# Output projection as one stage of all tokens, scaled up operands in DRAM, up products chained in PSUM, and an FFN without seams between its pieces

## The chip, the cores and the metric

One core of a Trainium2 chip runs the whole layer as one program. The metric is device microseconds of that core per execution; lower is better. The profile is of one execution, taken on the same core, and lists what every engine did: PE (matrix multiply; PEld is its weight load), DVE and ACT (elementwise work), POOL (GpSimd, elementwise work that cannot touch PSUM) and SP (which issues the DMAs).

## The reference

2048 prompt tokens and 32 sample tokens of width 1024 go through one layer, in float32:

```
n = rmsnorm(x);  z = n @ w_in
A = sliding-window attention with sinks,  B = gated linear attention (GLA)
h = x + concat(A, B) @ w_out                       # 1024 x 1024
y = h + relu(rmsnorm(h) * g_ffn @ w_up)^2 @ w_down # 1024 x 4096, 4096 x 1024
```

It also returns the last keys, values and GLA states.

## The kernel before

Every float32 matrix is split into a high part and the rest (h and l), and each product is three matmuls (`mm3`: h·h, h·l, l·h). Everything is transposed: channels lie on partitions and tokens on the free axis.

The program has an attention stage (`attention_phase`), a GLA stage (`gla_phase`) and an FFN stage (`ffn_phase`). Their order on PE is the program's order; tasks of the first two stages are interleaved by a clock of estimated PE time (`spawn`, `tick`). DMAs are issued from SP, in order, and an issue that waits holds those behind it.

The FFN stage works on three pieces of tokens with two groups each: 2 x 328, 2 x 356, 2 x 356. Both products of the FFN are done as 2 x 2 blocks with seven products instead of eight (Strassen-Winograd). The tokens' blocks are B11, B21 (group 0, channel halves), B22 and the differences T1 to T4; the weights' are A11, A12, A22 and sums S1 to S4. The hidden width of 4096 is cut into NF = 16 blocks of 256. Per block there are seven up products (`product`, 12 matmuls each), the relu and square, new differences of the hidden blocks (`uT1` to `uT4`), and seven down products (`down`, 12 matmuls each into two PSUM tiles, added by DVE to accumulators in SBUF at L1320). Down product i of block b-1 and up product i of block b alternate.

Per piece, in order: the output projection of its two groups (`op`, 192 matmuls per group; the first group of the first piece is done at the end of the GLA stage, in `prepare_ffn`), residual add, sums of squares, splitting into operands (`pair`), the 16 blocks, and then merges of the accumulators (`combine`, L1575) and stores. The RMS scale of each token is applied after the up products, in one DVE operation (L1488: max with 0, times scale). Each up product has its own PSUM tile, and DVE makes the sums and differences of products (L1320 with `r0`, `r1`, `r2`).

Weight pairs: `weights` (L1208) makes h on ACT and l on POOL from a staged load, for a ring of eight tiles, AHEAD = 7 steps before use. Pairs of w_down (and block 0 of w_up) are written to DRAM in the first piece and read back in the others; those of w_up are remade in every piece, with four POOL operations per block for the block sums (L1234). The output weights' pairs are written to DRAM once (L1305) and read in the two later pieces. In the later pieces POOL also makes five of the seven low parts of the hidden blocks (L1481).

The block sums of w_down are made ahead of the FFN by POOL (`down_sums`, L687 to L698): blocks 0 to 7 in the attention stage from its third tile on, blocks 8 to 15 in the GLA stage, in two tasks that load, add, store at once and then wait.

## Time and profile before

| | us |
|---|---|
| median of 3 runs (2425.57 to 2433.79) | 2426.84 |
| profiled execution | 2427.7 |
| its span, first to last instruction | 2425.7 |
| PE busy | 2211.6 |
| DVE busy | 1871.4 |
| POOL busy | 1426.5 |
| ACT busy | 1009.5 |
| mean granted TensorE clock | 0.960 of full |
| DMA | 437.49 MB, 180 GB/s |

Busy shares are averages over stages with different limits, so a stage is read by its own row, and a wait by what ended it. A line number is that of the kernel before; L42 and L135 are helpers through which all ACT operations and all matmuls go, so their groups are told apart by tile names: `dn` is a down product, `PS1T`, `PA12B` and the like are up products, `op` the output projection, `fB` hidden blocks, `sd` sums of w_down, `wf` weight pairs.

### The profile page before, as it was taken

How to read it: one execution, taken by the hardware profiler on the slowest of the kernel's cores; microseconds unless marked ns; L12 is line 12 of the kernel's file. 1: busy time of each engine (PE TensorE's matmuls, PEld its weight loads, DVE VectorE, ACT ScalarE, POOL GpSimd, SP SyncE). 2: the span in 40 equal slices, each digit the busy share in tenths (PEclk: the TensorE clock that was granted, in tenths of full speed). 3: DMA queues.
4: the chain of work that ended last, by engine and by line, in shares of the span. 5: the costliest groups of instructions: out<-in, count | busy, mean ns of one | idle time of the engine just before them, and what ended most of it. 6: DMA issues, size and time to landing. Idle time of an engine off the chain costs nothing.

```text
span 2425.7 us, 40665 instructions
## 1 busy us (share of the span) xinstructions
PE 2211.6 (91%) x14790; PEld 2038.2 (84%) x14790; DVE 1871.4 (77%) x3637; ACT 1009.5 (42%) x2197; POOL 1426.5 (59%) x1360
## 2 busy tenths in 40 slices
PE   7999999969988899999989799999999899999996
PEld 6776777758877789988889799999998789999995
DVE  8666766868985788888885578888886578888887
ACT  4444556536554544444442433333331443333331
POOL 6553225752333588887882366666674166666773
PEclk9999999889989899999999899999999899999998
DMA  9564455543157466565687355555558445555544
GB/s 304 185 204 149 163 176 180 191 163 110 61 195 227 153 220 228 217 217 217 217 300 240 114 168 166 163 163 163 165 165 250 155 153 165 158 164 157 165 133 133
DMA packets 259625, 437.49 MB, mean 180 GB/s; under 512 B 46289, under 2 KB 172546, under 8 KB 255586
## 3 DMA queue, kind: packets, MB, share of 16 engines
q1 hardware_dynamic: 259426, 434.90, 54.1%
q8 instruction: 117, 1.92, 0.3%
q14 instruction: 82, 0.67, 0.1%
HBM read 307.70 MB, written 127.13 MB: 179 GB/s over the span
## 4 chain that ended last, share of the span: by engine, by line
PE 51%; DVE 19%; POOL 11%; DMA 8%; issue 5%; ACT 4%; SPq 1%; DVEq 0%; ACTq 0%; POOLq 0%
PE dn L135 15%; DVE fB L1320 7%; PE op L135 6%; POOL stage L1234 4%; PE PA22T L135 3%; PE PS3T L135 3%; PE PS2T L135 3%; PE PS1T L135 3%; PE zv L135 3%; PE zq L135 3%; PE zr L135 2%; DMA sd<-sd 2%; DVE P L1320 2%; DMA sd<-in_w_down 2%; DVE y L1320 2%
## 5 line engine op out<-in xcount | busy, mean ns | idle before, releaser
L1320 DVE TENSOR_TENSOR y<-y,dn 128x712 f32<-128x712 f32 (+1 forms) x384 | 330.3, 868 | 11.9 <-PE dn L135 5.7
L1234 POOL TENSOR_TENSOR stage<-stage 128x512 f32<-128x512 f32 x184 | 249.0, 1353 | 12.1
L1320 DVE TENSOR_TENSOR P<-P,dn 128x712 f32<-128x712 f32 (+1 forms) x270 | 235.0, 871 | 27.1 <-PE dn L135 21.9
L1320 DVE TENSOR_TENSOR fB<-fB,fB 128x356 f32<-128x356 f32 (+1 forms) x192 | 204.2, 1063 | 4.9 <-ACT fB L42 2.9
L687 POOL TENSOR_TENSOR sd<-sd 128x128 f32<-128x128 f32 (+1 forms) x192 | 117.5, 628 | 66.4 <-DMA sd<-in_w_down 55.3
L912 POOL TENSOR_TENSOR E<-cc 128x256 f32<-128x256 f32 (+1 forms) x117 | 68.1, 621 | 81.4 <-DVE cc L764 79.6
L988 DVE COPY_PREDICATED AT<-masks,A 64x64 f32<-64x64 int32 (+1 forms) x330 | 82.6, 252 | 38.9 <-ACT AT L42 29.5
L1335 DVE TENSOR_TENSOR op<-op,y 128x356 f32<-128x356 f32 (+1 forms) x48 | 23.7, 523 | 84.2 <-PE op L135 36.0
L1346 POOL TENSOR_TENSOR sums<-sums,r 128x356 f32<-128x356 f32 (+1 forms) x9 | 8.4, 934 | 126.3 <-DVE sums L1346 85.8
L42 ACT ACTIVATE P<-S,negm 128x192 f32<-128x192 f32 (+2 forms) x128 | 51.6, 417 | 51.7 <-DVE negm L556 41.0
L1481 DVE TENSOR_TENSOR uT1l<-fB,uT1h 128x356 fp32r<-128x356 f32 (+1 forms) x48 | 69.7, 1452 | 0.0
L42 ACT ACTIVATE E<-E 128x1024 f32<-128x1024 f32 (+2 forms) x68 | 67.2, 1013 | 1.1
L1320 DVE TENSOR_TENSOR PA22T<-PA22T,r 128x356 f32<-128x356 f32 (+1 forms) x48 | 25.3, 527 | 53.0 <-PE PA22T L135 52.9
L42 ACT ACTIVATE y<-op 128x356 f32<-128x356 f32 (+1 forms) x48 | 22.3, 466 | 105.1 <-DVE op L1335 78.2
L42 ACT ACTIVATE uT2h<-fB 128x356 fp32r<-128x356 f32 (+1 forms) x48 | 23.6, 492 | 92.5 <-DVE fB L1320 92.5
L135 PE MATMUL op<-T3h,wf_o 128*128 128x356 f32 x128 | 38.4, 373 | 21.9 <-DVE T4l L1327 21.9
L923 DVE TENSOR_TENSOR E<-E,kq 128x256 f32<-128x256 f32 (+1 forms) x117 | 55.0, 522 | 2.0 <-ACT E L42 1.9
L42 ACT ACTIVATE uT1h<-fB 128x356 fp32r<-128x356 f32 (+1 forms) x48 | 23.8, 495 | 78.6 <-DVE fB L1320 78.6
L1320 DVE TENSOR_TENSOR r<-PS1T,r 128x356 f32<-128x356 f32 (+1 forms) x48 | 24.8, 516 | 41.1 <-PE PS1T L135 41.1
L1320 DVE TENSOR_TENSOR r<-PS3T,r 128x356 f32<-128x356 f32 (+1 forms) x48 | 24.8, 518 | 39.2 <-PE PS3T L135 39.2
L311 DVE TENSOR_TENSOR xT1a<-xT1a,packed 128x512 f32<-128x512 f32 (+2 forms) x36 | 22.4, 666 | 40.8 <-DMA xT1a<-in_xT_prompt 40.8
L42 ACT ACTIVATE fB<-PS1T 128x356 f32<-128x356 f32 (+1 forms) x48 | 22.1, 461 | 71.7 <-DVE PS1T L1488 71.7
(1861 smaller groups left out, 8864.4 us busy)
## 6 DMA issues: line engine op xcount, KB each, us to landing
stage<-in_w_up SPq DMA_DIRECT2D x92, 512.0 KB, 4.9
stage<-sd SPq DMA_DIRECT2D x32, 512.0 KB, 7.2
wf_o<-ko SPq DMA_DIRECT2D x32, 512.0 KB, 6.1
xT1a<-in_xT_prompt SPq DMA_DIRECT2D x16, 512.0 KB, 4.3
stage<-in_w_in SPq DMA_DIRECT2D x16, 512.0 KB, 5.3
sd<-in_w_down SPq DMA_DIRECT2D x64, 128.0 KB, 3.1
x1a<-in_x_prompt SPq DMA_DIRECT2D x16, 512.0 KB, 5.0
sd<-sd SPq DMA_DIRECT2D x32, 256.0 KB, 3.0
```

Source lines behind the costliest of these rows:

```text
L42: ins = f(*args, **kw)
L135: self._pe(self.T.matmul(out, lhsT, rhs, start=start, stop=stop), ns)
L311: V.tensor_tensor(out=xT[:, ks], in0=xT[:, ks], in1=self.gmix[:, ks].unsqueeze(2).broadcast_to([P, step, r]), op=ALU.mult)
L687: tt = lambda o, x, y, op: self.G.tensor_tensor(out=o, in0=x, in1=y, op=op)
L912: G.tensor_tensor(out=e4, in0=c4, in1=ref, op=ALU.subtract)
L923: V.tensor_tensor(out=e4, in0=e4, in1=halves_of(kq, L, m), op=ALU.mult)
L988: V.copy_predicated(dst, mk.unsqueeze(1).broadcast_to([L // nh, 2, w // m, m]), src[r].rearrange("s p (n m) -> s p n m", m=m),)
L1234: tt = lambda o, x, y, op: G.tensor_tensor(out=o, in0=x, in1=y, op=op)
L1320: tt = lambda out, x, y, op=ALU.add: V.tensor_tensor(out=out, in0=x, in1=y, op=op)
L1335: V.tensor_tensor(out=ps, in0=ps, in1=yf, op=ALU.add)
L1346: (G if pool else V).tensor_tensor(out=acc, in0=acc, in1=sq, op=ALU.add)
L1481: (G if pool else V).tensor_tensor(out=l, in0=src, in1=f32(h), op=ALU.subtract)
```

## The change

The output projection of all six groups becomes a stage of its own (`op_phase`) between GLA and FFN, with the output weights kept in SBUF. For each group it adds x, stores h to DRAM (`yd`), sums squares and, one group later (`post`), multiplies h by gain and scale, forms B11 to T4 and stores them to DRAM (`Td`). The same stage makes the sums of w_down for blocks 13 to 15 and sums of w_up for blocks 1 to 8, which it keeps in DRAM (`su`).

The FFN runs 3 x 16 blocks in one sequence, pieces in the order 1, 2, 0. Operands of the next piece are loaded and split (`load_tok`) as each up product of a piece's last block has been issued. Up products 0, 2, 4 and 6 accumulate in one PSUM bank (X) and 3 and 5 in another (W); ACT copies out what is needed in between. The RMS scale is already in the operands, so the relu is an ACT operation. All low parts of hidden blocks are made by DVE. The down order becomes A11, S4, S1, S3, S2, A12, A22. The residual h is loaded and added by POOL during blocks 2 to 9. Merges move partly into the last two blocks, and in pieces that are not the last they are on POOL.

Weight pairs of w_down are remade in every piece (only block 15 is kept, and block 0 of w_up as before); in the first piece two of seven are on DVE. Up sums that are kept are loaded instead of made; for blocks 9 to 15 the first half is kept in the first piece. The output weights are no longer written to DRAM.

`down_sums`: five blocks in the attention stage, from its tenth tile on, eight in the GLA stage; the store waits for the second pause and is put behind the DMA issued last before it.

```diff
--- before.py
+++ after.py
-EARLY = 8
-AHEAD = 7
+ORDER = (1, 2, 0)
+EARLY, MIDDLE = 5, 8
+AHEAD = 6
...
+        self.su = [[dt([P, KB // 2, 256], f"su{b}{j}") for j in range(2)] for b in range(self.NB)]
+        self.made = {}
+        self.Td = [
+            {x: dt([P, KB // 2, n], f"Td{p}{x}") for x in ("B11", "B21", "T2", "T1", "T3", "B22", "T4")}
+            for p, n in enumerate(sizes)
+        ]
...
-                if i == 2:
+                if i == 9:
...
-            a11, a21, a12, a22 = raw[:, 0, 0], raw[:, 0, 1], raw[:, 1, 0], raw[:, 1, 1]
-            tt(a22, a21, a22, ALU.add)
-            tt(a21, a11, a21, ALU.subtract)
-            tt(a11, a22, a11, ALU.subtract)
-            tt(a12, a12, a11, ALU.subtract)
-            self.Q.dma_start(self.sd[b][:, :, c0 : c0 + n], raw.rearrange("p k m n -> p (k m) n"))
+            self.block_sums(raw)
             yield gap / 2
+            with self.tc.issue_after(self.Q.last.ins):
+                self.Q.dma_start(self.sd[b][:, :, c0 : c0 + n], raw.rearrange("p k m n -> p (k m) n"))
...
-            late = [(b, c0, 256) for b in range(EARLY, self.NB) for c0 in (0, 256)]
+            late = [(b, c0, 256) for b in range(EARLY, EARLY + MIDDLE) for c0 in (0, 256)]
...
+        def post(p, gi, acc):
...
+            sc = rb[:, :N]
+            scaled = lambda out, f: V.scalar_tensor_tensor(out=out, in0=y[:, f], scalar=g(f), in1=sc, op0=ALU.mult, op1=ALU.mult)
+            Td = self.Td[p]
+            if gi == 0:
+                for f in range(KB):
+                    scaled(y[:, f], f)
+                    if f == H - 1:
+                        Q.dma_start(Td["B11"], y[:, :H])
+                Q.dma_start(Td["B21"], y[:, H:])
+                return
+            A, B = pa[:, :N], pb[:, :N]
...
+            for k in range(H):
+                scaled(A, k)
+                scaled(y[:, H + k], H + k)
+                tt(t3[:, k], y[:, H + k], A)
+                tt(A, A, y0[:, k])
+                S.activation(y[:, k], A, AF.Copy)
+                tt(B, y[:, H + k], A)
+                S.activation(t2[:, k], B, AF.Copy)
+                tt(t4[:, k], y0[:, H + k], B)
+            for x, src in (("T2", t2), ("T1", y[:, :H]), ("T3", t3), ("B22", y[:, H:]), ("T4", t4)):
+                Q.dma_start(Td[x], src)
...
+        todo, raws = [("d", b, c) for b in range(EARLY + MIDDLE, self.NB) for c in (0, 256)], []
+        todo += [("u", b, 0) for b in range(1, 9)]
...
+        for j, (p, gi) in enumerate(groups):
...
+            for f in range(KB):
+                if j == 0:
+                    ps = self.op0[f]
+                else:
+                    ps = self.ps_s(f"op{p}_{gi}_{f}")[:, :N]
+                    for kb in range(KB):
+                        w = [self.wo[f // H][kb // 4][x][:, kb % 4, cs] for x in range(2)]
+                        self.mm3(ps, *w, mix[p, gi](kb, 0), mix[p, gi](kb, 1), kb == 0, kb == KB - 1)
+                V.tensor_tensor(out=y[:, f], in0=ps, in1=y[:, f], op=ALU.add)
+                S.activation(ps if f else acc, y[:, f], AF.Square)
+                if f:
+                    V.tensor_tensor(out=acc, in0=acc, in1=ps, op=ALU.add)
+                if f % H == H - 1:
+                    hs = slice(f - H + 1, f + 1)
+                    Q.dma_start(self.yd[p][gi][:, hs], y[:, hs])
+                if f in (1, 2) and pending is not None:
+                    next(pending, None)
+                if f == (0 if gi else 2) and j + 1 < len(groups):
+                    load_y(*groups[j + 1])
+                if f == 1 and 2 <= j + 1 < len(groups):
+                    next_mix(*groups[j + 1])
+                if j and f in (1, 3, 5, 7):
+                    sums()
+            pending = post(p, gi, acc)
+        self.pending = pending
...
+            wring = [(wfb, i) for i in range(5)] + [(wfa, 0), (wfa, 1), (wfc, 0)]
...
+            def load_tok(e, x, engs):
+
+                h, l = e.T[x]
+                Q.dma_start(f32(l), self.Td[e.p][x])
+                for i, eng in enumerate(engs):
+                    ks = slice(i * H // len(engs), (i + 1) * H // len(engs))
+                    S.activation(h[:, ks], f32(l[:, ks]), AF.Copy)
+                    eng.tensor_tensor(out=l[:, ks], in0=f32(l[:, ks]), in1=f32(h[:, ks]), op=ALU.subtract)
...
+                def product(ps, i, first=False):
+
+                    w, t = UP[i]
+                    wh, wl = (x.rearrange("p (k c) -> p k c", k=H) for x in ws["U", g].pop(w))
+                    th, tl = e.T[t]
+                    for kb in range(H):
+                        self.mm3(ps, wh[:, kb], wl[:, kb], th[:, kb], tl[:, kb], first and kb == 0, kb == H - 1, skip_group_check=not first)
+                    if b == NF - 1 and n + 1 < len(envs):
+                        load_tok(envs[n + 1], t, (G, G))
...
+                X = bank(bx)
+                product(X, 0, True)
+                S.activation(r0, X, AF.Copy)
+                yield
+                Z = bank(bz)
+                product(Z, 1, True)
+                add(Z, Z, r0)
+                squared("B11", Z, f1)
+                yield
+                product(X, 2)
+                S.activation(r2, X, AF.Copy)
+                yield
+                W = bank(3)
+                product(W, 3, True)
+                S.activation(r5, W, AF.Copy)
+                yield
+                product(X, 4)
+                Y = bank(by)
+                add(Y, X, r5)
+                squared("B22", Y, f3)
+                yield
+                product(W, 5)
+                add(W, W, r2)
+                S.activation(W, W, AF.Relu)
+                S.activation(W, W, AF.Square)
+                add(Y, W, f1, ALU.subtract)
+                add(W, f3, W, ALU.subtract)
+                split("T1", Y)
+                split("T3", W)
+                add(W, W, f1)
+                split("T2", W)
+                yield
+                product(X, 6)
+                squared("B21", X, r5)
+                add(X, r5, W, ALU.subtract)
+                split("T4", X)
...
+            for x, g, i in steps:
+                if x == "U":
+                    if i == 0:
+                        ups[g] = up(g)
+                    next(ups[g])
+                    if g == 0 and i in (0, 2):
+                        next(self.pending, None)
+                else:
+                    down(g, i)
+                    n, b = divmod(g, NF)
+                    e, end = envs[n], n + 1 == len(envs)
+                    residual(g, i)
+                    if b == NF - 2 and i == 2:
+                        merge(e, 3, 5, False)
+                    if b == NF - 2 and i == 4:
+                        merge(e, 6, 1, False)
+                        merge(e, 2, 1, False)
+                    if b == NF - 1 and i == 4:
+                        merge(e, 3, 6, end)
+                        store(e, 3)
+                        merge(e, 7, 6, end)
+                        merge(e, 5, 7, end)
+                        store(e, 5)
+                    if b == NF - 1 and i == 5:
+                        store(e, 2)
+                    if b == NF - 1 and i == 6:
+                        merge(e, 4, 7, end)
+                        store(e, 4)
+                prepare()
```

More of the change, by code (lines that the diff above doesn't have):

```diff
@@ new lines, in up_weights, with fetch @@
+                raw = [None, None]
+                def fetch(k):
+                    raw[k] = load(w[:, H * k : H * k + H, 256 * b : 256 * b + 256])
+                half = lambda x, m: x[:, :, m * P : m * P + P]
+                tt = lambda o, x, y, op: G.tensor_tensor(out=o, in0=x, in1=y, op=op)
+                made = self.made.get(b, 0)
+                fetch(0)
+                if made < 2:
+                    fetch(1)
+                a11, a21 = half(raw[0], 0), half(raw[0], 1)
+                pair("A11", a11)
@@ L1242, in up_weights @@
+                yield
+                if made == 2:
+                    fetch(1)
+                a12, a22 = half(raw[1], 0), half(raw[1], 1)
+                sums = [load(x) for x in self.su[b][:made]]
+                pair("A12", a12)
                 yield
-                pair("A22", A(2, 2))
-                tt(A(2, 2), A(2, 1), A(2, 2), ALU.add)
-                if not b:
-                    pair("S1", A(2, 2))
+                if made:
+                    s2, s3 = half(sums[0], 0), half(sums[0], 1)
+                    pair("S2", s2)
@@ L1283, in down_weights @@
                 made = f"d{b}A11" in kept
+                src = {}
                 for i, (x, _, _) in enumerate(DOWN):
                     if not made and i == 0:
-                        fetch(0)
-                    if not made and i % 2 and i + 1 < 7:
-                        fetch(i + 1)
-                    out[x] = weights(f"d{b}{x}", lambda: halves[x], True)
-                    yield
-            def out_weights(fh):
-                kbs = []
-                for kb in range(KB):
-                    key = f"o{fh}{kb}"
-                    kbs.append(weights(key, None, True))
-                return kbs
@@ new lines, in down_weights @@
+                        src["A11"] = load(w_dn[b, :, 0:1, :512], True)
+                        s = load(self.sd[b][:, 2:4], True)
+                        src["S4"], src["S1"] = s[:, 0:1], s[:, 1:2]
+                    if not made and i == 2:
+                        s = load(self.sd[b][:, :2], True)
+                        src["S2"], src["S3"] = s[:, 0:1], s[:, 1:2]
+                    if not made and i == 4:
+                        s = load(w_dn[b, :, 1:2, :], True)
+                        src["A12"], src["A22"] = s[:, :, :512], s[:, :, 512:]
@@ new lines, in down_weights @@
+                    eng = V if n == 0 and i in (0, 5) else G
+                    out[x] = weights(f"d{b}{x}", None if made else src[x], keep, eng)
+                    yield
+            steps = [("U", 0, i) for i in range(7)]
+            total = len(envs) * NF
+            for g in range(1, total):
+                steps += [(x, g - (x == "D"), i) for i in range(7) for x in "DU"]
+            steps += [("D", total - 1, i) for i in range(7)]
+            ws, makers = {}, {}
+            todo = iter(steps)
@@ L1593, in ffn_phase, with merge @@
-                combine(6, 1)
-                combine(7, 6)
-                combine(6, 5)
-                combine(5, 7)
-                store(1, range(H, KB))
-                combine(3, 6)
-                store(1, range(H))
-                combine(4, 7)
-                store(0, range(H, KB))
-                if pi + 1 < len(pieces):
-                    y = [load_y(pi + 1, gi) for gi in range(2)]
+                            V.tensor_copy(at, ps)
+            def merge(e, q, x, last):
+                for j in range(0, H, 2):
+                    eng = V if last and j else G
+                    eng.tensor_tensor(out=e.acc[q][:, j : j + 2], in0=e.acc[q][:, j : j + 2], in1=e.acc[x][:, j : j + 2], op=ALU.add)
```

666 lines of the change are left out of this document (293 added, 373 removed).

## The prediction

> **What bounds the kernel now.** I read the busy shares, then the span cut by stage, then the chain of waits in one steady block, then waits by pair and single durations.
>
> ```profile
> span 2425.7 us, 40665 instructions
> PE 2211.6 (91%) x14790; PEld 2038.2 (84%) x14790; DVE 1871.4 (77%) x3637; ACT 1009.5 (42%) x2197; POOL 1426.5 (59%) x1360
> ```
>
> PE is the busiest engine, but where its idle time lies matters more than the 91%. The span by stage (columns: stretch, length, busy time of PE, weight loads, DVE, ACT, POOL, granted clock, DMA share, GB/s):
>
> ```profile
> core 0: us, PE busy (x) PEld busy (x) DVE busy (x) ACT busy (x) POOL busy (x), PEclk, DMA share, GB/s
> 505.00:530.00 25.00, 4.29 (x116) 3.35 (x114) 4.55 (x12) 3.47 (x9) 10.94 (x15) 0.66 0.66 225
> 690.00:718.00 28.00, 20.93 (x195) 18.03 (x193) 25.20 (x70) 16.12 (x27) 9.79 (x4) 0.76 0.88 293
> 797.90:1278.00 480.10, 436.16 (x2716) 420.46 (x2715) 417.08 (x605) 224.47 (x453) 391.74 (x293) 0.96 0.62 223
> 1278.00:1363.70 85.70, 72.23 (x392) 70.31 (x393) 39.83 (x65) 25.07 (x56) 20.79 (x17) 0.88 0.53 169
> 1363.70:1847.80 484.10, 458.03 (x2722) 445.25 (x2721) 395.19 (x522) 168.94 (x334) 326.56 (x266) 0.98 0.54 171
> 1847.80:1928.50 80.70, 68.80 (x394) 67.86 (x393) 41.48 (x67) 25.15 (x56) 12.25 (x8) 0.92 0.52 172
> 1928.50:2407.70 479.20, 455.10 (x2712) 441.36 (x2710) 393.18 (x519) 161.98 (x318) 312.08 (x252) 0.99 0.50 158
> 2407.70:2425.70 18.00, 0.03 (x1) 0.00 (x0) 10.59 (x7) 0.00 (x0) 9.41 (x5) 0.58 0.38 122
> 1427.15:1456.26 29.11, 27.89 (x168) 27.27 (x169) 24.27 (x32) 9.73 (x19) 20.05 (x16) 1.00 0.52 164
> 1875.00:1899.80 24.80, 24.80 (x153) 24.50 (x151) 15.18 (x29) 13.62 (x32) 0.00 (x0) 1.00 0.61 235
> ```
>
> The rows are: a hole in the GLA stage; its end; then FFN, seam (the output projection of a piece), FFN, seam, FFN; the tail; one steady block; the densest stretch of a seam. Clock and holes go together: stretches with PE nearly full are granted 1.00, those with holes 0.66 to 0.92, so a hole costs itself and a slow restart.
>
> Inside a steady block the chain of waits runs through products back to back, then leaves PE:
>
> ```profile
> 1516.86 1.95 PE PS2T L135 x12
> ```
> ```profile
> 1530.69 0.65 ACT wf_u6A L42
> 1531.41 1.31 POOL wf_u6A L1208
> 1532.79 1.31 POOL stage L1234
> 1534.16 1.29 POOL stage L1234
> 1535.46 0.92 POOL uB22l L1481
> 1536.38 1.62 DVE fB L1320
> ...
> 1542.67 0.51 ACT uT2h L42
> ```
> ```profile
> PE dn L135 <- ACT uT2h L42: 17.0, 14, 1.2
> ```
> ```profile
> PE dn L135 <- DVE y L1320: 29.3, 27, 2.2
> ```
> ```profile
> 902.98 1.81 PE dn L135 x12
> ```
>
> Twelve matmuls of 356 columns take 1.95 us, of 328 columns 1.81 us. A block is 14 such products, 27.3 us dense, but its period is 29.11: weight copy on ACT, four GpSimd operations, DVE differences, uT2, and PE waits 1.2 us for it (14 blocks: 17.0). In the first piece the wait is for DVE's accumulation (29.3 in 27 waits).
>
> **The change, part by part.** Base: from the first matmul of the second output group to the last product, all PE work as if back to back.
>
> ```profile
> 753.86 0.41 PE L135 MATMUL op<-m1h,wo00h 128*128 128x328 f32 x1 [0.53 <-ACT op L42]
> ```
> ```profile
> 1381.17 2.02 PE rb L135 x8
> ```
>
> The number of matmuls is unchanged. FFN: 2 x 16 x 27.3 + 16 x 14 x 1.81 = 1279.0. Five output groups of 16 twelves each: 4 x 31.2 + 29.0 = 153.8. The row-scale broadcasts, now six: 6 x 2.02 = 12.1. With 753.9 in front: 2198.8. Before, the same work ended at 2407.7, so 209 us of holes are at stake, and the tail.
>
> *Up products chained, scale moved to the tokens.* DVE did 17 operations per block in later pieces (22 in the first), among them two-SBUF ones:
>
> ```profile
> L1320 DVE TENSOR_TENSOR y<-y,dn 128x712 f32<-128x712 f32 x256 | 224.9, 889 | 8.3 <-PE dn L135 2.6
> ...
> L1320 DVE TENSOR_TENSOR fB<-fB,fB 128x356 f32<-128x356 f32 x128 | 140.8, 1100 | 4.5 <-ACT fB L42 2.9 <-POOL B22l L1083 1.3
> ...
> L1320 DVE TENSOR_TENSOR PA22T<-PA22T,r 128x356 f32<-128x356 f32 x32 | 17.2, 537 | 36.1 <-PE PA22T L135 36.1
> ...
> L1575 POOL TENSOR_TENSOR y<-y,P 128x356 f32<-128x356 f32 x8 | 14.0, 1773 | 1.4 <-DVE y L1320 1.3
> ```
>
> Now it does 14, each with a PSUM operand: 14 x 0.537 + 14 x 0.889 = 20.0 us of 27.3. A difference with both operands in SBUF took 1100 ns, one with a PSUM operand 537. The Trainium skill (SBUF — State Buffer, "Who interferes with whom") says that a DVE instruction with two SBUF inputs and a GpSimd instruction that reads SBUF exclude each other for the whole instruction, and that one SBUF input does not contend; the two rows agree, and by that rule alone the in-block waits below would be nothing and the result 29 us lower.
> ACT: 21 operations at the 0.51 of uT2 + 14 weight copies x 0.65 = 19.8 us. GpSimd: 14 low parts x 1.31 = 18.3, up to 5.2 for block sums and 3.7 for the residual (two 712-wide additions at 1.31/512 per element = 1.82 each): at most 27, usually 20 to 24. All fit under 27.3, none by much. New waits: the next product on bank X waits for ACT's copy of it, but two down products and another up product (5.9 us) lie between; behind it on PE everything queues. uT1 is made after the sixth up product and needed five products (9.8 us) later; to it lead an addition, two ACT passes, a difference and the split, 3.6 us plus what queues on DVE. I take 0.6 us of wait per block, half the 1.2 of the row: 48 x 0.6 = 29; bounds 0 and 58.
>
> *Down sums paced.*
>
> ```profile
> L691 SPq DMA_DIRECT2D sd<-in_w_down x32: 539/592/612, 397.0 to 511.9; - x32
> ```
> ```profile
> PE go L135 <- ACT kdT L42: 19.7, 1, 19.7
> ```
> ```profile
> 521.01 5.72 DMA g<-rgd
> ```
> ```profile
> 702.77 6.68 DMA m<-mixT
> ```
>
> The sixteen units of the GLA stage bunch into 397 to 519 us; the gate load waits behind them on SP until 521.0, ACT waits for it, and PE idles 19.7. The store is now tied to its place behind the previous DMA, which spreads them. The same tie can hold the next load behind a store, so the gain is between 0 and 20.7 (25.00 less 4.29); I take 20, since the work itself does not grow. The copies of the output weights to DRAM, issued from SP ahead of the mixer load at 702.77, vanish: of 7.1 idle there I take 5 (0 to 7.1). Twelve of the 32 small units leave the attention stage; I take nothing for it.
>
> *Weight pairs recomputed instead of kept.* Per block 3.5 MB written (first piece) or read (later) become 1.75 MB read. The price is the GpSimd and ACT work counted above.
>
> *Output projection as a stage.* Its DMA, from the shapes: x and h of six groups 8.5 + 8.5 MB, mixer outputs 5.8, scaled operands 14.9, down sums that leave the earlier stages 6.3, up sums now made once and kept 16.8: 60.8 MB beside 153.8 + 10 us of PE. The steady block moves 164 GB/s at share 0.52 and the seam stretch 235 at 0.61, that is 315 to 385 at full share: 193 to 158 us. The sums are issued on the queue that brings x and the next mixer output. I take 15 us; bounds 0 and 40. The Trainium skill (DMA: Bandwidth & Descriptors, "Measured") gives 425 GB/s for a 16 MB load of a core alone and about 358 with its neighbour streaming; an estimate by it is 143 or 170 us, so a wait of 0 to 6 in place of my 15, and no row here reaches those rates.
>
> *No seams.* Loading and splitting the next piece's operands goes under the last block's products. GpSimd takes 14 halves x 1.82 = 25 us, the merges 14 x 1.82 = 25 us, and the weight pairs 5 x 1.31 + 14 x 1.31 = 25: 75 us in two slots of 27.3 at the first join, about 66 at the second (its d15 pairs are kept, its operands shorter). That is 21 and 12 over; six steps of lead cover 11.7 each, which leaves about 10, my value; bounds 0 and 33, the latter if the lead is already used up. The first piece still loads two operands after the last projection matmul, since their memory holds its input: 6.7 us to land, as the mixer load above, plus about 4 of splitting, less the two products before them (3.9), is 7; with the scale chain I take 8; bounds 0 and 20.
>
> *Tail.* Before, 18.0, with six merges after the last accumulation.
>
> ```profile
> 2413.37 8.59 SPq L1569 DMA_DIRECT2D out_yT_prompt<-y  x12
> ```
>
> Now one merge follows: addition 0.89, merge 1.82, four issues at 0.72 (8.59 / 12), and 3.7 from the last issue to the end as here (2413.37 + 8.59 to 2425.7): 9.3, with a little queueing 10; bounds 6 and 18.
>
> Sum: 2198.8 + 29 + 15 + 8 + 10 + 10 - 25 = 2245.8 for the span; 2.0 lies around it in the profiled execution (2427.7 against 2425.7), which stands 0.9 above the median 2426.84: **2247**. All ends low 2178, all high 2369.
>
> **Rivals.**
> *DMA paces the projection stage.* Three groups in the middle move about 40 MB in 94 us, 430 GB/s, above anything in the rows. If mixer loads queue behind the sums the bound of 40 is paid: 2272. Against: the last group has almost no DMA, and loads run one group ahead.
> *GpSimd sets the block.* It has 18 to 27 us per block and waits in order for ACT, which waits for loads. If the period stays 29.1 (27.3 + 1.8), 48 x 1.8 = 86 replaces 29: 2304; with the full 33 at the joins 2327. For it: GpSimd was on the chain before at only 20.05 of 29.11.
> *Slower.* GpSimd on every weight pair in all pieces, at the price it shows while DVE runs SBUF operations: 1773 ns for 356 columns is 2.55 us a pair, 14 x 2.55 = 35.7 us per block. Outside the blocks the sum is 939, so it decides above (2426.8 - 939) / 48 = 31.0 us per block, 2.2 us per pair; at 35.7 the time is 2653. Against: DVE keeps no two-SBUF operation in the block but two splits in the first piece.
>
> **How the numbers follow.** Forecast 0.66 (its own range 2205 to 2300), DMA 0.11, GpSimd 0.14, slower 0.05, better than 2205 0.04. From 2205 to 2330 it holds about 0.86: all but the slower rival, what is better, and the upper part of the GpSimd case. About 0.3% (7 us) is what a measurement can tell from no change; only the slower rival and a sliver beside it reach that, so faster 0.93, same 0.02, slower 0.05.
>
> **What would show it.** PE rows in FFN stretches within 1 us of full per block and clock 1.00 throughout; a period of 27.3 to 28.0 (25.3 to 26.0 in the 328 piece); no row at clock under 0.9 after about 740 us; projection stage 165 to 190 us; no PE wait on kdT near 500; under 12 us after the last matmul. Wrong if the period is 29 or more, if PE waits on low parts from GpSimd in every block, or if the hole in GLA only moves.

## The result, and the profile after

| | us |
|---|---|
| before, median of 4 runs on the same chip | 2426.4 |
| after, median of 4 runs (2278.04 to 2290.66) | 2285.31 |
| ratio, with its 95% interval | 0.941 (0.9377 to 0.9443) |
| profiled execution of after, its span | 2278.04, 2276.1 |

The change makes the kernel 5.9% faster. The time is 38 us above the 2247 of the forecast and inside its range. Of these, 30.3 lie in the span (2276.1 against 2245.8). The other 8.2 come from the median: the profiled execution is the lowest of the four and stands 7.3 below it, where the forecast had 0.9 above.

The first lines of the page of after:

```profile
span 2276.1 us, 40775 instructions
PE 2139.4 (94%) x14790; PEld 2007.6 (88%) x14790; DVE 1577.8 (69%) x3444; ACT 1230.9 (54%) x2728; POOL 1436.6 (63%) x1308
```

DVE lost 294 us of work. PE has as many matmuls as before and is busy 72 us less, since fewer of them run at a slow clock. The span by stage, columns as in the forecast's table of stretches:

```profile
505.00:530.00 25.00, 23.98 (x194) 20.20 (x194) 22.53 (x78) 11.38 (x17) 14.59 (x23) 1.00 0.33 110
731.40:899.90 168.50, 163.68 (x1042) 163.04 (x1040) 88.84 (x222) 42.53 (x83) 79.82 (x66) 0.99 0.94 317
899.90:1000.00 100.10, 47.95 (x254) 46.32 (x253) 37.28 (x71) 43.97 (x85) 53.50 (x41) 0.69 0.66 246
1000.00:1027.30 27.30, 27.30 (x170) 27.30 (x169) 19.98 (x30) 16.40 (x36) 15.48 (x13) 1.00 0.45 139
1027.30:1354.00 326.70, 326.70 (x2010) 326.70 (x2010) 245.14 (x359) 196.91 (x419) 236.30 (x181) 1.00 0.46 145
1354.00:1440.00 86.00, 75.33 (x446) 74.07 (x445) 62.99 (x81) 52.00 (x105) 80.09 (x55) 0.96 0.72 252
1440.00:1822.00 382.00, 382.00 (x2351) 382.00 (x2350) 259.41 (x388) 232.22 (x493) 292.05 (x225) 1.00 0.48 149
1822.00:1860.00 38.00, 35.59 (x223) 35.08 (x222) 26.63 (x39) 21.37 (x44) 34.90 (x23) 1.00 0.91 338
1860.00:2240.00 380.00, 379.13 (x2527) 378.87 (x2527) 259.49 (x415) 239.79 (x528) 318.53 (x245) 1.00 0.49 154
2266.40:2276.10 9.70, 0.07 (x1) 0.00 (x0) 1.91 (x2) 0.00 (x0) 1.35 (x1) 0.50 0.46 141
```

Row 1 is where PE was busy 4.29 of 25 before: the hole is closed. Row 2 is the projection stage: the DMA engines are 0.94 busy for 168.5 us and PE hardly waits. Rows 4, 5, 7 and 9 are FFN blocks, without a gap but for 0.9 us in row 9: the 29.11 us of a block became 27.3, the dense value. What is left to win is in row 3: the first 100 us of the FFN, in which PE works 48, at a clock of 0.69. The joins (rows 6 and 8) and the tail (row 10) are small.

Who keeps PE waiting in row 3, and ACT, from the waits by pair of after (us in total, times, longest):

```profile
PE u L156 <- ACT wf_u0A L43: 37.9, 1, 37.9
PE dn L156 <- ACT wf_d0A L43: 13.8, 1, 13.8
```
```profile
ACT wf_u0A L43 <- DMA su<-stage: 14.3, 1, 14.3
ACT T2h L43 <- DMA T2l<-Td1T: 8.7, 1, 8.7
ACT T3h L43 <- DMA T3l<-Td1T: 3.3, 1, 3.3
```

The first up product waits for its weight tile, and ACT can't write that tile until `su<-stage` has landed, the store of a sum of w_up. The two have no data in common. But the FFN's ring of weight tiles (`wfb`) is allocated where the projection stage had its staging tiles for the sums (`opx`). The timeline shows why the stores are late: SP issues the last four only from 928.29 on, behind GpSimd's sums.

```profile
927.01 7.59 POOL L1161 TENSOR_TENSOR stage<-stage 128x512 f32<-128x512 f32 x6
```
```profile
928.29 6.66 SPq L59 DMA_DIRECT2D su<-stage  x4
```
```profile
938.04 0.67 PE L156 MATMUL u<-B11h,wf_u0A 128*128 128x356 f32 x1 [37.94 <-ACT wf_u0A L43]
```

The sums should have ended inside the stage, whose last matmul starts at 899.8; with the DMA engines 0.94 busy they slipped past it.

### The profile page after: what moved, and what is told of

Read it like the earlier page. It is cut to its first block, busy times and chain, and to the rows that moved or that the text cites. A ratio compares the mean times of both kernels' runs of the same rounds, so it can differ in the third digit from the quotient of the medians.

```text
span 2276.1 us, 40775 instructions
## 1 busy us (share of the span) xinstructions
PE 2139.4 (94%) x14790; PEld 2007.6 (88%) x14790; DVE 1577.8 (69%) x3444; ACT 1230.9 (54%) x2728; POOL 1436.6 (63%) x1308
## 4 chain that ended last, share of the span: by engine, by line
PE 54%; DVE 2%; DMA 2%; POOL 1%; ACT 0%; issue 0%; SPq 0%; ACTq 0%; POOLq 0%
PE dn L156 27%; PE u L156 27%; DVE P L1509 1%; DVE wf_d15A L1391 0%; DMA B22l<-Td2B 0%; DMA T3l<-Td0T 0%; DMA stage<-in_w_down 0%; DVE P L1609 0%; DMA Td2T<-y 0%; DMA ku0S<-wf_u0S 0%; DMA stage<-sd 0%; DVE u L1509 0%; POOL wf_u0S L1391 0%; DMA su<-stage 0%; POOL stage L1416 0%
## 5 line engine op out<-in xcount | busy, mean ns | idle before, releaser
L1509 DVE TENSOR_TENSOR P<-P,dn 128x712 f32<-128x712 f32 (+1 forms) x642 | 559.7, 875 | 234.7 <-PE dn L156 218.6
L43 ACT ACTIVATE u<-u 128x356 f32<-128x356 f32 (+1 forms) x384 | 174.1, 454 | 38.3 <-PE u L156 22.0
L707 POOL TENSOR_TENSOR sd<-sd 128x256 f32<-128x256 f32 (+1 forms) x168 | 110.7, 668 | 99.7 <-DMA sd<-in_w_down 93.4
L43 ACT ACTIVATE r<-u 128x356 f32<-128x356 f32 (+1 forms) x192 | 88.4, 461 | 136.3 <-PE u L156 136.2
L1509 DVE TENSOR_TENSOR u<-u,r 128x356 f32<-128x356 f32 (+1 forms) x144 | 75.7, 526 | 117.3 <-PE u L156 115.4
L1609 POOL TENSOR_TENSOR P<-P,P 128x712 f32<-128x712 f32 (+1 forms) x38 | 64.9, 1728 | 26.3 <-DVE P L1509 26.1
L1161 POOL TENSOR_TENSOR stage<-stage 128x512 f32<-128x512 f32 x32 | 42.9, 1344 | 43.0 <-DMA Td1T<-y 21.6
L1416 POOL TENSOR_TENSOR stage<-stage 128x512 f32<-128x512 f32 x44 | 57.0, 1294 | 10.4 <-DMA stage<-in_w_up 5.0
L576 DVE TENSOR_REDUCE mx<-S 128x2 f32<-128x384 f32 (+2 forms) x64 | 32.7, 536 | 26.8 <-PE S L156 26.5
L1509 DVE TENSOR_TENSOR u<-u,f 128x356 f32<-128x356 f32 (+1 forms) x96 | 49.8, 519 | 0.3 <-ACT u L43 0.2
L156 PE MATMUL u<-B11h,wf_u0A 128*128 128x356 f32 (+1 forms) x24 | 7.8, 392 | 38.3 <-ACT wf_u0A L43 37.9
L43 ACT ACTIVATE f<-u 128x356 f32<-128x356 f32 (+1 forms) x96 | 43.7, 455 | 0.0
```

The costliest lines, as they stand in the source:

```text
L43: ins = f(*args, **kw)
L156: self._pe(self.T.matmul(out, lhsT, rhs, start=start, stop=stop, **kw), ns)
L576: V.reduce_max(mx[:, ch, us], sp, axis=AX.X)
L707: tt = lambda o, x, y, op: self.G.tensor_tensor(out=o, in0=x, in1=y, op=op)
L1161: tt = lambda o, x, y, op: self.G.tensor_tensor(out=o, in0=x, in1=y, op=op)
L1416: tt = lambda o, x, y, op: G.tensor_tensor(out=o, in0=x, in1=y, op=op)
```

## The experiments

Two kernels are best compared from the end of the projection stage to the end of the span, because the stages before vary by themselves: in after and the eight kernels here whose instructions are the same up to there, the second output group starts anywhere from 729.2 to 744.8. The mark taken is the last matmul `op<-mx1l,wo10h`, called the last projection matmul below; it starts 2.1 us before the stage's very last one in each of these kernels. The kernels were measured on several chips; the medians of the kernel before, measured beside them, lie between 2426.4 and 2430.1. The stretch from the mark on, with the PE waits in its first 100 us (the two longest, or the sum and then the wait of the first down product):

| kernel | median us | last projection matmul starts at | from there to the end | PE waits at the FFN's start |
|---|---|---|---|---|
| after | 2285.31 | 897.7 | 1378.4 | 37.9 + 13.8 |
| no up sums | 2260.43 | 909.3 | 1349.0 | 22.1, of them 12.7 for `wf_d0A` |
| up sums of four blocks | 2256.1 | 895.0 | 1353.2 | 19.3, 10.9 |
| copies in place of the sums | 2253.26 | 896.1 | 1353.0 | 19.4, 12.5 |
| store at once | 2283.05 | 910.8 | 1372.8 | 31.5 + 14.1 |
| low parts on GpSimd | 2302.77 | 903.6 | 1395.3 | 38.1 + 13.3 |
| low parts from SBUF | 2296.38 | 908.4 | 1390.0 | 38.1 + 13.6 |
| joins with DVE | 2285.15 | 901.2 | 1380.5 | 37.4 + 13.5 |
| DVE loaded | 2281.91 (1 run) | 896.9 | 1383.2 | 38.1 + 13.2 |
| half, general staging | 2253.41 | 902.5 | 1349.8 | 20.7, 12.9 |
| early sums | 2241.11 | 893.0 | 1346.6 | 21.2, 13.4 |
| early sums, ring skips a tile | 2241.11 | 897.6 | 1346.0 | 20.2, 9.2 + 3.4 |

**What holds up the start of the FFN.** Theory: the memory of the weight tiles, held by unfinished sums. Rivals: the reload of T2 and T1, which the forecast had in mind, and the volume of the DMA.

No up sums in the projection stage:

```diff
-        todo += [("u", b, 0) for b in range(1, 9)]
+        todo += [("u", b, 0) for b in range(1, 1)]
```

> The projection stage makes no sums of w_up; blocks 1 to 8 then make them in the FFN, as blocks 9 to 15 do already. In the profile of the changed kernel PE idles 52.2 us in the 100 us behind the projection stage (37.9 for a weight copy on ACT that waits for the stores of the sums, 13.8 for one that waits for the stores of the last group's operands). Memory theory: the first weight tiles of the FFN lie in the memory in which the sums are staged, so without sums the 37.9 become the 8.7 us that T2 takes to arrive and its split, about 10, and the second wait stays: idle about 24, time lower by 28 to 40 than 2285, some of it the clock. GpSimd gets 4 x 1.3 us more in eight blocks, which stay dense as blocks 9 to 15 are. Load theory (T2 and T1, loaded only after the last projection matmul, set the start): idle stays over 40 and the time within 8 us of 2285. DMA theory (the volume of the sums delays all that is loaded there): as by the memory theory in this run.

Four blocks, the same line with `range(1, 5)`:

> Sums of w_up for four blocks in place of eight. Memory theory: what counts is that the last sums are stored before the projection stage ends; ten of twenty places are used, so they are done, and this runs as without sums: idle about 24, time lower by 28 to 40 than 2285. DMA theory: half the volume, half the gain: idle about 38, time lower by about 17. Load theory: no change.

The same stretch of the first and of the second (100 us from 900), and the waits of PE in the first:

```profile
900.00:1000.00 100.00, 77.93 (x464) 75.51 (x464) 58.40 (x105) 54.88 (x111) 56.66 (x42) 0.91 0.49 173
```
```profile
900.00:1000.00 100.00, 83.02 (x462) 80.56 (x463) 63.12 (x111) 60.61 (x124) 52.52 (x38) 0.88 0.55 196
```
```profile
PE dn L156 <- ACT wf_d0A L43: 12.7, 1, 12.7
PE u L156 <- POOL T4l L1507: 2.6, 1, 2.6
PE u L156 <- issue: 2.3, 1, 2.3
```

The 37.9 are gone in both: 464 and 462 matmuls in the 100 us where after had 253. T2, the forecast's suspect, costs 3.1 us with four blocks. Half the sums do as well as none: what counts is that they end in time. In their medians the two gain 25 and 29 us, where 28 to 40 were expected; from the last projection matmul on it is 29.4 and 25.2.

To separate volume from memory, DRAM-to-DRAM transfers of the same bytes took the place of the eight sums:

```diff
-                x = self.up_raw(b, extra)
-                self.up_sums(x)
+                w = a["w_up"].rearrange("(k p) n -> p k n", p=P)
+                for k in range(2):
+                    cp = self.dram.tile([P, H, 256], F32, tag=f"cp{b}{k}", name=f"cp{b}{k}")
+                    Q.dma_start(cp, w[:, H * k : H * k + H, 256 * b : 256 * b + 256])
+                return
```

> In place of the eight up sums of the projection stage, 16 transfers of 512 KB from DRAM to DRAM at the same places of the program, whose result nobody reads: the same bytes read and written, but no staging memory and no GpSimd work. Memory theory: the start is as without sums, idle about 24, time lower by 25 to 40 than 2285. DMA theory: idle stays at 45 or more and the time within 10 us of 2285, since T2 and the weights arrive as late as with the sums.

This one told nothing on its question: without an operand to wait for, the copies were issued in the first 130 us (242 GB/s there against 188 in after), and the projection stage moved 290 GB/s from 760 to 900, where after moved 324. The median of 2275.24 gains only 10 us, because the copies cost the stages before: the first product of the GLA stage starts at 401.8 in place of 384.7, the second output group at 758.7 in place of 731.4. So the copies were tied to their place by `with tc.issue_after(Q.last.ins):`

> As the run with 16 transfers of 512 KB from DRAM to DRAM in place of the eight up sums, but each tied behind the DMA before it, since untied they were issued in the first 130 us and left no load in the projection stage. Memory theory: waits of PE in the 100 us behind the projection stage about 22 us, as without sums (22.1 there), though the bytes are those of the kernel with all the sums (51.7 there). DMA theory: 45 or more.

The projection stage (from 760) and the start of the FFN with the copies in place:

```profile
760.00:900.00 140.00, 138.53 (x880) 138.22 (x878) 72.58 (x179) 38.79 (x74) 52.78 (x41) 1.00 0.98 336
900.00:1000.00 100.00, 81.96 (x475) 79.95 (x476) 64.65 (x114) 62.09 (x128) 68.47 (x51) 0.90 0.50 178
```

A DMA share of 0.98 at 336 GB/s, more than after's 0.93 at 324 in that stretch, and the start is as without sums: waits of 19.4 us, 32 us off the median. The volume is not it; the staged sums are, with the GpSimd work and the memory that go with them.

These runs don't part the memory from the GpSimd work. In after the chain through the memory is the one that ends last: GpSimd ends the sums at 934.6 (927.01 + 7.59), the last store lands, ACT writes the weight tile at 937.37. But GpSimd makes the low part of the same weights only behind those sums, at 938.07, and the third matmul of the first product needs it. A kernel with separate memory and the same order on GpSimd would therefore start only some 3.5 us earlier (an estimate from these rows, not tried). What the runs show is that late sums hold the start.

**The second wait, for `wf_d0A`.** It stays at 11 to 13 us without up sums, with four blocks of them and with copies in place. First guess: the FFN's own staging tiles lie under operands of the last group.

```diff
-                        src["A11"] = load(w_dn[b, :, 0:1, :512], True)
+                        src["A11"] = load(w_dn[b, :, 0:1, :512], n or b)
```

(and so for the other three loads, with sums for four blocks)

> Sums of w_up for four blocks, and the loads for the first block's down weights go to the general staging tiles, not to the FFN's own, whose memory holds the last group's operands until their stores have landed. With four blocks of sums alone PE waits 19.3 us behind the projection stage, 10.9 of it for that copy on ACT. If memory is what it waits for, the 10.9 fall under 3 and the time is 6 to 10 below 2256, about 2248. Rival: the first down products wait for something else just as late (operands T2, T4, the first hidden blocks, or loads queued on SP), and the time is within 4 us of 2256.

The guess fell: 12.9 us, time within 3 of 2256. ACT waits there for `Td2T<-y` as before, though the staging tile is another one. That leaves the destination: `wf_d0A` is the eighth weight tile, `wfc`, which reaches into the memory of the last group's y. The next kernel moves it, on top of the early sums told further down:

```diff
-                p, i = wring[count["w"] % len(wring)]
+                k = count["w"]
+                p, i = wring[k if k < 7 else (k - 7) % len(wring)]
```

> As the run with the sums of w_down early, and the ring of weight tiles skips its eighth tile in the first round: that tile lies in the memory of the last group's y, and the first down weight (A11 of block 0) had to wait there until y was stored; now it takes the tile of the first up weight, which is free after one product. Memory theory, refined: moving the staging tiles changed nothing because it is the weight tile itself; so the wait of the first down product, 13.4 us with the early sums, falls under 4, part of it may come back at the fourth down product, whose operand uT3 lies where the last group's T tiles are stored from; time 6 to 12 below 2241, about 2232. Rival: the first down product waits for the work of the last group's operands on ACT and DVE, which stands ahead of it in their queues; then 10 or more stays and the time is within 4 us of 2241.

Both medians are 2241.11. The waits of PE:

```profile
PE dn L156 <- DVE tT L1237: 9.2, 1, 9.2
PE dn L156 <- ACT P L43: 3.4, 1, 3.4
```

The wait on the weight tile is gone, and 12.6 of its 13.4 us are back with two other releasers. The first is DVE, making the last group's T operands; PSUM tiles of that stage lie, as I read the code, where the down products write (argued, not tried). So the rival was right in what counts: the last group's `post`, which runs beside the first up products, bounds this wait, and the tile was only the last of several to come free.

**The pacing of the sums of w_down.** The old store, at once and untied:

```diff
-            yield gap / 2
-            with self.tc.issue_after(self.Q.last.ins):
-                self.Q.dma_start(self.sd[b][:, :, c0 : c0 + n], raw.rearrange("p k m n -> p (k m) n"))
+            self.Q.dma_start(self.sd[b][:, :, c0 : c0 + n], raw.rearrange("p k m n -> p (k m) n"))
+            yield gap / 2
```

> The sums of w_down are stored at once after they are made and without the tie to the DMA before, as in the kernel before; the number of units and all else stay. If the pacing is what closed the hole near 500 us (forecast 20 us of gain), the hole comes back: PE idles 15 to 21 us more in the GLA stage, and the first matmul of the second output group comes at 745 to 752 in place of 731.4, time higher by 14 to 21. If the hole went because there are fewer and later units (rival), the time is within 5 us of 2285.

The stretch and the wait in this kernel:

```profile
500.00:530.00 30.00, 8.99 (x151) 8.15 (x151) 7.36 (x20) 6.06 (x13) 19.59 (x28) 0.67 0.73 240
```
```profile
PE go L156 <- ACT kdT L43: 21.0, 1, 21.0
```

It is the hole of before (19.7 on the same wait), and no kernel with the paced store has it. The second output group starts at 749.8: 18.4 later than in after's profile, 14 later than the mean of the nine kernels with the same instructions (735.5), 5 later than the latest of them. Yet the median is 2283.05, no later than after's 2285.31, where 14 to 21 more were expected. In the profiles 18.4 became 7.5 by the end: the projection stage ran 5 us shorter and the first up product waited 31.5 in place of 37.9. While the start of the FFN waits for late sums, time won before it is partly waited away there.

The attention stage, with all its units back and none in the projection stage:

```diff
-EARLY, MIDDLE = 5, 8
+EARLY, MIDDLE = 8, 8
...
-                if i == 9:
+                if i == 2:
```

> Sums of w_down for blocks 0 to 7 in the attention stage from its third tile on, as in the kernel before, and none in the projection stage; the pacing of the stores and the eight up sums stay. After the change the GLA stage's first product came at 384.7 us, before it at 396.1. If the twelve small units taken out of the attention stage gave those 11 us (the forecast took nothing for them), it comes at 393 to 397 here; if not, at 383 to 388. Memory theory for the start of the FFN: with six units fewer the up sums end before the projection stage does, so the 51.7 us of PE waits there fall to 20 to 30. Sum: 2285 + 10 - 27 = about 2268; if the attention stage is indifferent, about 2258.

The GLA stage's first product comes at 390.3 (384.7 after, 396.1 before; 392.7 in the kernel told above with the same units): they cost the attention stage 5.6 to 8 of the 11 us, between the two expectations. The other part may be the pacing: with the old store and after's units the product comes at 389.4. Neither size is sharp, since in the nine kernels with after's attention stage it comes at 382.1 to 387.5. The third output group starts at 763.9 against 766.8 (765.9 to 780.2 in the nine), so nothing of that is left by then. And without six units in the projection stage the wait for the up sums is gone, though all eight are there:

```profile
760.00:900.00 140.00, 137.69 (x868) 137.41 (x867) 72.76 (x178) 37.55 (x72) 70.96 (x49) 0.99 0.96 341
900.00:1000.00 100.00, 81.15 (x471) 79.40 (x470) 64.91 (x114) 62.11 (x127) 52.99 (x39) 0.89 0.54 192
```

The time is 2241.11, ratio to before 0.9235 (0.921 to 0.9261): better than both kernels, with two numbers changed. That is 17 below the lower expectation: the stretch from the last projection matmul on is 31.8 us shorter than in after, the stages before it 4.7, and the profiled execution of after from which I reckoned stands 7.3 below its own median.

**Why no wait is left inside the blocks.** Three suspects were put back singly. First the low parts of three hidden blocks, on GpSimd:

```diff
-                    S.activation(ps, ps, AF.Square)
-                    add(l, ps, f32(h), ALU.subtract)
+                    G.tensor_tensor(out=l, in0=out, in1=f32(h), op=ALU.subtract)
```

> The low parts of the three squared hidden blocks (B11, B22, B21) go back to GpSimd, from the copy in SBUF that the next sums use anyway; ACT makes one copy less for each. Everything else as after the change. GpSimd gets 3 x 0.9 us per block more, in all about 18 to 24 of 27.3. Chain theory (the waits inside the blocks before the change came from the GpSimd queue standing between product and product, and moving this work to DVE removed them): PE waits come back at 0.5 to 1.5 us per block, 48 x 1 = about 48 us longer, waits of the down products on uB22l, uB21l. Capacity theory (an engine binds only when it is full, and none is): the period stays 27.3 and the time within 6 us of 2285. The rival of the forecast, in which GpSimd sets the block, asks for a period of 28 or more.

Then on DVE, but from SBUF: the last line as `add(l, out, f32(h), ALU.subtract)`.

> The same three low parts stay on DVE but are taken from the copy in SBUF in place of PSUM, so that both operands of the difference lie in SBUF; ACT makes one copy less for each. Before the change a difference of this shape took 1100 ns with both operands in SBUF and 537 with one in PSUM. If the operands' place is what makes that difference, these three take 0.9 to 1.1 us, those left 0.52, and GpSimd's weight pairs (1.29) get longer; DVE goes from 18.7 to about 20.4 of 27.3 us per block and the time stays within 5 us of 2285, since DVE has the room. If instead a price of the queue or the shape made the 1100, they take 0.52.

Then more work for DVE, behind up products 0, 2 and 3:

```diff
+                    if n and 2 <= b < 14 and i in (0, 2, 3):
+                        s = idle["s"]
+                        for _ in range(4):
+                            add(s[:, :256], ps[:, :256], s[:, 256:])
```

> In blocks 2 to 13 of the second and third piece DVE does twelve additions of 256 columns more per block (PSUM plus SBUF into a tile that nobody reads), right after the up products 0, 2 and 3; an estimate from 0.52 us for 356 columns is 0.39 each, 4.7 us per block. DVE goes from 18.7 to about 23.4 of 27.3 us per block, 0.86; before the change it was at 24.27 of 29.11, 0.83, with PE waits of 1.2 us per block. Load theory (the waits inside the blocks went because DVE got lighter, 0.69): waits come back, 0.5 to 1.5 us per block, the 24 blocks 12 to 36 us longer. Slack theory (the new order leaves every result several products of time, so that an engine under full does not show): the period stays at 27.3 and 25.3 and the time within 8 us of 2285.

The same stretch of the second piece in after and in these three, in this order:

```profile
1450.00:1820.00 370.00, 370.00 (x2277) 370.00 (x2276) 256.21 (x383) 223.66 (x477) 282.03 (x217) 1.00 0.47 145
```
```profile
1450.00:1820.00 370.00, 367.25 (x2257) 366.80 (x2256) 229.37 (x328) 210.91 (x432) 319.37 (x260) 1.00 0.48 149
```
```profile
1450.00:1820.00 370.00, 370.00 (x2277) 369.95 (x2276) 283.91 (x378) 213.88 (x437) 284.79 (x217) 1.00 0.48 147
```
```profile
1450.00:1820.00 370.00, 370.00 (x2277) 370.00 (x2276) 302.46 (x528) 224.80 (x476) 282.31 (x217) 1.00 0.47 146
```

PE stays full with GpSimd at 0.86, with two-SBUF differences on DVE, and with DVE at 0.82 (before the change it was 0.83 with waits). The 2.75 us of the second row belong to the first join, which ends later there. So in this piece none of the three by itself holds PE up, and the rival that GpSimd sets the block is ruled out up to 0.86 x 27.3 = 23.6 us. Where the first two lose time (17 and 12 us from the last projection matmul on) is mostly outside the blocks: GpSimd's load shows at the first join, 17.8 us of PE waits in place of 10.5, and the SBUF differences at the second, where PE waits 6.9 us in one place.

The traces show one mechanism in both. In the first piece DVE makes two weight pairs per block, with both operands in SBUF; where nothing holds it up such a pair takes 0.68 us. With the low parts on GpSimd three of them take 4.2 to 4.3 us, while GpSimd works without a pause, and PE waits 0.7 to 0.9 us right behind each, inside blocks:

```profile
1208.10 4.23 DVE L1391 TENSOR_TENSOR wf_d8A<-stage,wf_d8A 128x512 fp32r<-128x512 f32 x1
1213.62 0.43 PE L156 MATMUL dn<-uT3h,wf_d8S 128*128 128x356 f32 x1 [0.74 <-DVE P L1509]
```

In the kernel with differences from SBUF one of these takes 11.56 us at the second join, and the 6.9 us of PE lie behind it. So GpSimd's load and two-SBUF operations on DVE can bring waits together where neither engine is full; no run put both back. (The profile of the SBUF kernel ends 22.3 us after that of after, but 10.7 of that lie before the last projection matmul, where its instructions are the same; of this below.)

**The joins.** DVE takes half of the split:

```diff
-                        load_tok(envs[n + 1], t, (G, G))
+                        load_tok(envs[n + 1], t, (V, G))
```

> At the two joins between pieces DVE splits one half of each operand of the next piece in place of GpSimd doing both: 7 x 1.8 = 12.6 us less for GpSimd at each join. In the profile of the changed kernel PE waits 10.5 us at the first join (1340 to 1450 us), 7.1 of it in one wait for an accumulation on DVE. GpSimd theory (the joins are long because GpSimd is full): 10.5 falls under 4, the second join's 4 too, time lower by 6 to 10. Rival (DVE's accumulation waits for a merge on GpSimd or for its own queue): the 7.1 stays or grows, since DVE has 7 operations more, and the time is within 4 us of 2285.

The first join in this kernel:

```profile
PE dn L156 <- DVE P L1509: 4.3, 4, 1.8
PE dn L156 <- POOL wf_d0S L1391: 3.2, 1, 3.2
PE dn L156 <- ACT r L43: 0.6, 1, 0.6
```

8.1 us in place of 10.5: the long wait of 7.1 went and others came. The second join lost 1.7 (PE busy 45.9 of 50 us against 47.6), and the time is the same, 2285.15. What the 7.1 was stands in the trace of after:

```profile
1401.17 9.38 DVE L1391 TENSOR_TENSOR wf_d15A<-stage,wf_d15A 128x512 fp32r<-128x512 f32 x1
1408.72 1.28 POOL L1391 TENSOR_TENSOR wf_d0A<-stage,wf_d0A 128x512 fp32r<-128x512 f32 x1
1411.41 0.67 PE L156 MATMUL dn<-uT2h,wf_d15S 128*128 128x356 f32 x1 [7.13 <-DVE P L1509]
```

A weight pair on DVE takes 9.38 us in place of 0.68. It ends at 1410.55, just after the last of a row of GpSimd instructions (1408.72 + 1.28 = 1410.00); the accumulation that PE waits for stands behind it on DVE. The same pair takes 8.6 to 11.0 us in every kernel of the table but two. One of these is this kernel, in which GpSimd has pauses (84.8 busy of the 100 us from 1350, 92.0 in after): here the pair takes at most 1.84. So the GpSimd theory was right about this wait, though not by GpSimd's own lateness. That the seven operations added on DVE brought the other waits is argued from their place alone.

## Why the forecast was right, and where it was off

| term | forecast | measured |
|---|---|---|
| second output group starts (gains in GLA included) | 728.9 | 731.4 |
| projection stage to its last matmul, five broadcasts | 178.9, of it 15 waits | 168.5, of it 4.8 |
| start of the FFN | 8 | 59 |
| waits inside the blocks | 29 | 0 |
| two joins | 10 | 15.3 |
| last block | no term | 6.8 |
| tail | 10 | 9.7 |

The 59 are 52.15 us of idle PE and 7 of slow clock: the 254 instructions of the stretch would take 41 at full speed and took 47.95. The joins are counted so too: 86.0 - 446 x 0.1625 = 13.5 and 38.0 - 223 x 0.1625 = 1.8. The differences add to +26 of the +30.3 in the span; about 4 stay unassigned. That the time fell into the range is partly luck: the start of the FFN came out 51 too long, the waits inside the blocks and the projection stage 29 and 10 too short.

**Right.** The base held: a period of 27.3 in the 356 pieces and 25.2 in the other (168 x 379.13 / 2527), with PE full. The hole in the GLA stage went by the pacing, as said, and comes back without it. The tail came out at 9.7, though by other terms: its last merge is on DVE and takes 1.07 in place of 1.82, and thirteen issues follow from 2267.20 on in place of four, among them those of the sample tokens.

**Wrong: "with the scale chain I take 8; bounds 0 and 20".** The step asked which operands have their memory under the projection stage's input, and found T2 and T1. It did not ask it of the weight tiles, which lie under the staging of the sums, nor what GpSimd has in front of their low parts. The real price of 51.7 us of waits is beyond the bound. The cause stood in another term: the forecast had the sums on a saturated queue and expected them to stall PE inside the stage (15, bounds 0 and 40). PE waited 4.8 there; the sums slipped behind the stage instead, where they held the first weights up.

**Wrong size: the waits inside the blocks, 29 for 0.** The lower bound was the truth. Why the old waits went is not settled: in the second piece three suspects singly don't bring them back. Two causes are left: the order (more products between a result and its use), and GpSimd's load together with two-SBUF operations on DVE. Both are argued, not tried, though the three waits of the first piece above are of the second kind. The Trainium skill (SBUF — State Buffer, "Who interferes with whom") would have given nothing for these waits, through the removal of two-SBUF operations; the number is right, but the run with such operations put back has no waits in the second piece either, so they alone are not the reason.

**Near by another cause: the joins, 10 for 15.3.** The forecast had GpSimd's work run over the two slots. At the first join 7.1 of the 10.5 us of waits come from the weight pair on DVE instead, which it had named ("two splits in the first piece") and given no price. In the last block, which had no term, PE waits 3.5 of the 6.8 us behind two merges on DVE.

**Wrong by what was left out, and near by luck: the 25.** The attention stage got shorter by 11.4 us, for which the forecast took nothing; about half of it comes from the units moved away. The GLA stage, from its first product to the second output group, gave 11.1 and not 25. The wait of 19.7 is gone, but PE's idle time in the stage fell only from 35.8 to 26.8: other waits grew, such as 5.6 for `cc`, which is new, and 9.5 in place of 6.9 for `AT`. The 5 taken for the output weights' copies are not there: at the same instructions PE is busy 20.67 of 28 us (670 to 698), before 20.93, and its waits there, before and after, are for DVE's `AT` and `g` and not for the mixer load. Both stages together are near the 25 taken.

**The rivals.** DMA did not pace the projection stage, GpSimd did not set the block, and the kernel did not become slower. "No row at clock under 0.9 after about 740" failed with the 0.69 at the start of the FFN, which was the sign named for it.

## What to carry to other kernels

When a new stage takes over memory, ask for each first tile of the stage whose last use it waits for; a background task whose result is needed much later can still be the one that holds the memory, or the queue, needed first. Background work beside a saturated resource didn't slow the main work here, it slipped behind it: give it a place where it surely ends, or less of it. Time won ahead of such a wait doesn't arrive in full until the wait is gone. And look for single long instructions where an engine is full: one DVE operation with both operands in SBUF held PE for 7 us.

## What the runs showed of the hardware

- The GLA stage is not of one length. The kernel without up sums issues the same instructions in the same order as after, on every engine, up to the projection stage, but its third output group starts at 780.2 and after's at 766.8. The rows below (after, then without up sums) go from the first product of the stage to that group. The same matmuls keep PE busy 6.7 us longer, at a clock of 0.93 in place of 0.96, and the waits are 6.8 longer: half of the 13 us each. Why the clock differs is not shown; the Trainium skill (TensorE: Matmul & The Clock Gate, "Part 1: The HAM clock gate") calls its window free-running and the ramp run-variable, which fits these two rows.

```profile
384.70:766.80 382.10, 352.06 (x3835) 305.49 (x3833) 307.75 (x947) 201.11 (x374) 185.52 (x239) 0.96 0.49 156
```
```profile
384.60:780.20 395.60, 358.79 (x3834) 311.76 (x3833) 307.84 (x947) 200.77 (x374) 181.15 (x239) 0.93 0.47 151
```

- A DVE difference with both operands in SBUF took 521 to 1924 ns (medians 1153 and 1633 for `uB22l` and `uB11l`) beside a busy GpSimd, where the one with a PSUM operand took 521 throughout. Two took far longer, 9.10 us at 1447.25 and 11.56 at 1888.48, as did the weight pair of after with 9.38. Each of the three began while GpSimd worked, GpSimd began six to eight more instructions meanwhile, and each ended within 0.6 us of GpSimd's next pause. GpSimd's weight pairs mostly kept their 1.29 us (means of four 1.29 to 1.44): it is DVE that pays. Groups of the kernel with low parts from SBUF, in the second piece from 1460 on (durations are least, median and most):

```profile
L1509 DVE TENSOR_TENSOR uB11l<-f,uB11h x13: 654/1633/1924, 1474.1 to 1802.1; 128x356 fp32r<-128x356 f32 x13
L1391 POOL TENSOR_TENSOR wf_d2S<-stage,wf_d2S x4: 1288/1292/1298, 1481.9 to 1493.6; 128x512 fp32r<-128x512 f32 x4
```

- The projection stage moves 317 GB/s at a DMA share of 0.94 for 168.5 us, loads and stores mixed, with 4.8 us of PE idle. The most that a kernel here moved in that stage is 343 GB/s, at a share of 0.96, from 760 to 900 with early sums and a skipped tile; my estimate of 430 GB/s in the middle was never reached, and the sums slipped.
